# Attention scores: the correction product on 64 rows of the array, two heads on its two row halves

## The chip, the cores and the metric

The kernel runs on one core of a Trainium2 chip. Its time is the device time of one execution in microseconds (us); the median of three executions stands for the kernel. The profiled execution has a time of its own, which lies near that median.

The engines are named as in the profile: PE is TensorE's matmul and PEld its load of the stationary operand, DVE is VectorE, ACT is ScalarE, POOL is GpSimd, SP issues most DMAs.

## The reference, cut to what matters

The model has two layers over 256 latent and 256 context tokens of width 1024. Each layer has a mixer of three branches (attention, a state-space scan, retention) and an MLP. The change concerns the attention branch: 8 query heads of width 64, in two groups of four, and each group shares one key and one value head.

```python
q = rms_norm(aq.reshape(b, l, ATTN_HEADS, ATTN_HEAD_DIM), q_norm)      # then rotary, for latent tokens
s = jnp.einsum('bqkgd,bskd->bkgqs', qblk, k, preferred_element_type=jnp.float32) * scale
p = jax.nn.softmax(s, axis=-1).astype(v.dtype)
return jnp.einsum('bkgqs,bskd->bqkgd', p, v)
```

Context tokens attend to the 256 context tokens, latent tokens to all 512. Layer 0 computes all four blocks of 128 query tokens, layer 1 (the last) only the two latent blocks.

## The kernel before, in words

All matrix products take their operands as two parts, a high part rounded to fp32r and the low part that remains. A weight product is then three matmuls (high x high, low x high, high x low), at lines L256 to L258 and, for the projection of q, L268 to L270. These make up most of TensorE's work.

For the scores the two parts of a query head (64 + 64 values) are put on the 128 rows of the array together. `prep_q` (L540) rounds q (L555, ACT), subtracts (L556, DVE), and transposes the pair through the array (L559) to `qT_`: for each head 64 rows of high part and, below them, 64 rows of low part. `prep_k` lays the keys' high part twice over each other (`kT_[:, g, 0]`), and likewise their low part (`kT_[:, g, 1]`). So a head's scores for a block of 128 queries are two matmuls (L633) into one PSUM bank, both on all 128 rows: the first is (q high + q low) x k high, the second (q high + q low) x k low.

`att(g)` (L612) runs one group. A step is one PSUM bank of 512 score columns: one head with 512 keys, or two heads (`u` = 0, 1) with 256 keys. For each step `front` (L628) issues the matmuls, DVE takes the row maximum (L636), ACT the exponential (L640), DVE the division (L645). `back` transposes the probabilities through the array (L655) and ACT copies them to SBUF (L657, L659). `value` multiplies them with v (L670): two heads at a time on the two column halves of the array, 64 columns each (`tile_position=(0, 64 * j)`), in plain f32. The loop at L677 issues `front` of step n, `value` of step n - 4, `back` of step n - 3.

PSUM has eight banks: three rotate under the name `gps` for the weight products, four under `mps` for everything in attention, one is `xps`.

The order of the instructions on each engine is not that of the code. A scheduler places them when the program is built: by the order in which they were issued, by its own reckoning of when operands and buffers are ready, and so that TensorE always has something; between the steps of attention it puts weight products (z, the second q, x). At run time each engine goes through its list in that fixed order.

The places that the change touches: the split of q at L555 and L556, the list of steps at L624 and L625, and the matmuls of `front` at L630 to L634.

Of the kernel before, what the change touches and what calls it, by code (L numbers as in the profile page):

```python
# [10 lines left out]
F32R = mybir.dt.float32r  # L11
I32 = mybir.dt.int32
AF = mybir.ActivationFunctionType
ALU = mybir.AluOpType
# [78 lines left out]
def build(nc, tc, h0, cc, cr, wm, wg, wt, wk, ws, cols, rep, cst, cst2, out, taps=None):  # L93
    taps = taps or {}
    ctx = ExitStack()
    with ctx:
# [8 lines left out]
        V, A, PE = nc.vector, nc.scalar, nc.tensor  # L105
# [5 lines left out]
        def gps(shape):  # L111
            return gp.tile([P, 512], F32, tag="g", name="gps")
# [4 lines left out]
        def mps():  # L117
            return mp.tile([P, 512], F32, tag="m", name="mps")
# [25 lines left out]
        def rpv(l, nm):  # L144
            o, w = REPS[nm]
            return rp[:, l * NREP + o:l * NREP + o + w]
# [74 lines left out]
        def split(hi, lo, src):  # L221
            W["cp"] = A.copy(hi, src)  # L222
            return V.tensor_tensor(lo, src, hi.bitcast(F32), ALU.subtract)  # L223
# [131 lines left out]
        with tc.tile_pool(name="st", bufs=1, reuse_waits="tile") as stp:  # L355
# [33 lines left out]
            ps = mps()  # L389
# [55 lines left out]
        for l in range(DEPTH):  # L445
# [8 lines left out]
            with ExitStack() as lctx:  # L454
# [6 lines left out]
                def bt(shape, tag, bufs=1, dt=F32):  # L461
                    return bp.tile(shape, dt, tag=tag, name=tag, bufs=bufs)

                def mt(shape, name, dt=F32):
                    n = 4 * math.prod(shape[1:])
                    c = 4 if n > 2048 else 2 if n > 1024 else 1
                    return bp.tile(shape, dt, tag=f"m{c}", name=name, bufs=NB[c])

                def art(n, name, dt=F32):
                    return bp.tile([P, n], dt, tag="ar", name=name, bufs=2)  # L470
# [8 lines left out]
                kT_ = art(2048, "kT", F32R).rearrange("p (g x s) -> p g x s", g=2, x=2)  # L479
                qT_ = cp.tile([P, 8, T], F32R, tag="hm", name="qT")  # L480
# [59 lines left out]
                def prep_q(g, i, rsq):  # L540
                    ps = qps[g][i]
                    pv = ps.rearrange("p (a b c) -> p a b c", a=2, b=4)
                    sq = mt([P, 8, 64], "sqq")
                    A.activation(sq, ps.rearrange("p (a c) -> p a c", a=8), AF.Square)
                    V.reduce_sum(rsq[:, 8 * i:8 * i + 8], sq, AX.X)
                    qr = mt([P, 2, 4, 64], "qr")
                    if qt[2 * i] < 2:
                        V.tensor_tensor(qr.rearrange("p a b c -> p (a b) c"), pv.rearrange("p a b c -> p (a b) c"),
                                        rpv(l, "qn").unsqueeze(1).to_broadcast([P, 8, 64]), ALU.mult)
                    else:  # L550
                        t2 = mt([P, 2, 4, 64], "t2")
                        rope64(pv, cw[:, 0], 4, sq.rearrange("p (a b) c -> p a b c", a=2), t2, qr)
                    for a_ in range(2):
                        q2 = mt([P, 4, 2, 64], "q2")
                        A.copy(q2[:, :, 0, :].bitcast(F32R), qr[:, a_])  # L555
                        V.tensor_tensor(q2[:, :, 1, :].bitcast(F32R), qr[:, a_], q2[:, :, 0, :], ALU.subtract)  # L556
                        ps = mps()
                        for j in range(4):
                            PE.transpose(ps[:, j * 128:j * 128 + 128], q2[:, j].rearrange("p a b -> p (a b)"), ident)  # L559
                        o = (2 * i + a_) * 128  # L560
                        A.copy(qT_[:, 4 * g:4 * g + 4, o:o + 128], ps.rearrange("p (j s) -> p j s", j=4))
# [27 lines left out]
                ps = mps()  # L589
# [22 lines left out]
                def att(g):  # L612
                    rsq = bt([P, 16], "rsq")
                    for i in range(nt // 2):
                        prep_q(g, i, rsq)
                    sq_, rsq = rsq, bt([P, 16], "rsr", 2)
                    nsc = bt([P, 16], "nsc", 2)
                    rsqrt(rsq[:, 0:4 * nt], sq_[:, 0:4 * nt], nsc[:, 0:4 * nt], 1.0, 64 * EPS)
                    V.tensor_scalar(nsc[:, 0:4 * nt], rsq[:, 0:4 * nt], -1.0, None, ALU.mult)
                    steps = []  # L620
                    for i in range(nt):
                        nk = 256 if qt[i] < 2 else 512
                        nh = 512 // nk
                        for jp in range(2):  # L624
                            steps += [(i, jp, s_, nk, nh) for s_ in range(2 // nh)]  # L625
                    st = {}

                    def front(i, jp, s_, nk, nh):  # L628
                        j0 = 2 * jp + s_
                        ps = mps()  # L630
                        for u in range(nh):
                            for x in range(2):
                                PE.matmul(ps[:, u * nk:u * nk + nk], qT_[:, 4 * g + j0 + u, i * 128:i * 128 + 128],  # L633
                                          kT_[:, g, x, 0:nk], start=x == 0, stop=x == 1)  # L634
                        mx = bt([P, 8], "mx", 6)
                        V.reduce_max(mx[:, 0:nh], ps.rearrange("p (u k) -> p u k", u=nh), AX.X)  # L636
                        V.tensor_tensor(mx[:, 2:2 + nh], mx[:, 0:nh], nsc[:, 4 * i + j0:4 * i + j0 + nh], ALU.mult)
                        pr = mt([P, T], "pr")
                        for u in range(nh):
                            A.activation(pr[:, u * nk:u * nk + nk], ps[:, u * nk:u * nk + nk], AF.Exp,  # L640
                                         bias=mx[:, 2 + u:3 + u], scale=rsq[:, 4 * i + j0 + u:4 * i + j0 + u + 1],
                                         accum_out=mx[:, 4 + u:5 + u])
                        V.reciprocal(mx[:, 6:6 + nh], mx[:, 4:4 + nh])
                        for u in range(nh):
                            V.tensor_scalar(pr[:, u * nk:u * nk + nk], pr[:, u * nk:u * nk + nk],  # L645
                                            mx[:, 6 + u:7 + u], None, ALU.mult)
                        st[i, jp, s_] = pr

                    def back(i, jp, s_, nk, nh):
                        if s_ == 0:  # L650
                            st["pT", jp] = mt([P, 4, 2, 128], "pT")
                        pT, pr = st["pT", jp], st.pop((i, jp, s_))
                        pt = mps()
                        for c in range(4):
                            PE.transpose(pt[:, c * 128:c * 128 + 128], pr[:, c * 128:c * 128 + 128], ident)  # L655
                        if nh == 1:
                            A.copy(pT[:, :, s_], pt.rearrange("p (c s) -> p c s", s=128))  # L657
                        else:
                            A.copy(pT[:, 0:2].rearrange("p c u s -> p u c s"),  # L659
                                   pt.rearrange("p (u c s) -> p u c s", u=2, c=2))  # L660
                        return pT

                    def value(i, jp, s_, nk, nh):
                        ncn = nk // 128
                        if s_ < 2 // nh - 1 or jp == 0:
                            return
                        po = mps()[:, 0:256]
                        for c in range(ncn):
                            for j in range(2):
                                PE.matmul(po[64 * j:64 * j + 64], vt[:, c, 64 * g:64 * g + 64],  # L670
                                          st["pT", j][:, c].rearrange("p u s -> p (u s)"), start=c == 0, stop=c == ncn - 1,
                                          tile_position=(0, 64 * j))
                        split(brh[:, 2 * g:2 * g + 2, i * 128:i * 128 + 128],
                              brl[:, 2 * g:2 * g + 2, i * 128:i * 128 + 128],
                              po.rearrange("p (u s) -> p u s", u=2))

                    for n in range(len(steps) + ALAG + VLAG):  # L677
                        if n < len(steps):
                            front(*steps[n])
                        if n >= ALAG + VLAG:  # L680
                            value(*steps[n - ALAG - VLAG])
                        if ALAG <= n < len(steps) + ALAG:
                            back(*steps[n - ALAG])
# [398 lines left out]
            with ExitStack() as lctx:  # L1082
# [35 lines left out]
                for i in range(7):  # L1118
                    ps = gps(None)
# [39 lines left out]
                for half in range(2):  # L1159
# [11 lines left out]
                    for i in range(i0, 16):  # L1171
                        ps = gps(None)
# [3 lines left out]
                    for i in range(8):  # L1176
# [18 lines left out]
                        else:  # L1195
                            ps = gps(None)
                            for kk in range(2):
                                fm(l, ("w2", half, i, kk), hhf[kk][0], hhf[kk][1], 8, ps[:, 0:nq],
                                   start=kk == 0, stop=kk == 1)
# [138 lines left out]
```

## Time and profile before

| | before |
|---|---|
| median of 3 executions | 1448.71 us (1448.47 to 1449.59) |
| profiled execution, its own time | 1447.74 us |
| span of its trace | 1445.9 us |
| PE busy | 1430.7 us, 99% of the span |
| DVE busy | 1011.8 us, 70% |
| ACT busy | 664.4 us, 46% |
| chain that ended last, by engine | PE 94%, DVE 3%, DMA 1%, ACT 1% |

The span runs from the first to the last instruction; what lies around it is 1.8 us. A matmul's duration in the trace is longer than the time after which the next one starts, since matmuls are pipelined. What a matmul costs in a row of them is therefore read from the distance between two starts and not from its duration, and a PE that is called busy can still be waiting for some tenths of a microsecond.

### The profile page before, as it was taken

To read this page: it belongs to the slowest core of one execution; us is meant where nothing else is said; L and a number is where in the kernel's file an instruction comes from. 1 tells how busy PE (TensorE), PEld (TensorE's weight loads), DVE (VectorE), ACT (ScalarE), POOL (GpSimd) and SP (SyncE) were. 2 spreads that over 40 slices of the span, in tenths; PEclk is the share of its full clock that TensorE was granted. 3 is DMA by queue.
4 is the path that set the end of the run, shared out by engine and by line. 5 is a ranking of instruction groups with operands and counts; after the bars stand their busy time and mean duration, and the time that the engine had idled before them with its cause. 6 is when DMAs were issued, how large, how long until landed. Compare 5 with 4: busy or idle time off the path is not lost.

```text
span 1445.9 us, 22592 instructions
## 1 busy us (share of the span) xinstructions
PE 1430.7 (99%) x8790; PEld 1236.2 (85%) x8790; DVE 1011.8 (70%) x2003; ACT 664.4 (46%) x1170; POOL 61.9 (4%) x118
## 2 busy tenths in 40 slices
PE   8999999999999999999999999999999999999997
PEld 6877777888888889888888888987988999999997
DVE  5778589598866767895456644797985876765664
ACT  4577567242322335442224323576663444663563
POOL 0000010000000000000001100000000020000000
PEclk9999999999999999999999999999999999999999
DMA  9411344354025582564545634232443466655551
GB/s 355 184 45 44 102 121 107 125 180 161 30 95 167 165 315 75 174 214 136 161 156 192 195 115 139 88 123 73 140 132 102 132 228 222 207 189 181 186 188 60
DMA packets 66107, 217.07 MB, mean 150 GB/s; under 512 B 7600, under 2 KB 10032, under 8 KB 65872
## 3 DMA queue, kind: packets, MB, share of 16 engines
q1 hardware_dynamic: 53264, 170.99, 35.4%
q0 software_dynamic: 12736, 44.64, 9.8%
q8 instruction: 69, 1.13, 0.3%
q14 instruction: 38, 0.31, 0.1%
HBM read 213.44 MB, written 2.16 MB: 149 GB/s over the span
## 4 chain that ended last, share of the span: by engine, by line
PE 94%; DVE 3%; DMA 1%; ACT 1%; issue 0%; SPq 0%; DVEq 0%
PE gps L258 23%; PE gps L256 23%; PE gps L257 23%; PE mps L951 2%; PE mps L953 2%; PE mps L952 2%; PE mps L670 2%; PE mps L633 1%; PE mps L655 1%; DMA R<-drow 1%; PE mps L765 1%; PE gps L951 1%; PE gps L952 1%; PE gps L953 1%; PE mps L975 1%; DVE wl L223 1%
## 5 line engine op out<-in xcount | busy, mean ns | idle before, releaser
L222 ACT CAST wh<-raw 128x1024 fp32r<-128x1024 f32 (+1 forms) x284 | 297.3, 1049 | 554.2 <-PE gps L257 452.8
L223 DVE TENSOR_TENSOR wl<-raw,wh 128x1024 fp32r<-128x1024 f32 (+1 forms) x284 | 347.2, 1225 | 236.8 <-ACT wh L222 235.2
L256 PE MATMUL gps<-uh,wh 128*128 128x256 f32 (+1 forms) x1304 | 442.5, 340 | 0.6 <-DVE sz L691 0.3
L258 PE MATMUL gps<-uh,wl 128*128 128x256 f32 (+1 forms) x1304 | 442.6, 340 | 0.1
L257 PE MATMUL gps<-ul,wh 128*128 128x256 f32 (+1 forms) x1304 | 442.3, 339 | 0.0
L256 PEld LDWEIGHTS gps<-uh,wh 128*128 128x128 f32 x1304 | 246.4, 189 | 28.1 <-issue 1.5
L258 PEld LDWEIGHTS gps<-uh,wl 128*128 128x128 f32 x1304 | 246.7, 189 | 27.6 <-issue 2.1
L257 PEld LDWEIGHTS gps<-ul,wh 128*128 128x128 f32 x1304 | 246.6, 189 | 26.5 <-issue 0.7
L258 PE MATMUL gps<-hh__5331,wl 128*128 128x512 f32 (+1 forms) x272 | 102.6, 377 | 0.0
L256 PE MATMUL gps<-hh__5331,wh 128*128 128x512 f32 (+1 forms) x272 | 102.5, 377 | 0.0
L257 PE MATMUL gps<-hl__5332,wh 128*128 128x512 f32 (+1 forms) x272 | 102.4, 377 | 0.0
L216 DVE CUSTOM_DVE_ANT_0 mraw<-mraw,crow,cl 128x1024 f32<-128x1024 f32 x64 | 82.0, 1282 | 1.1
L1104 DVE SCALAR_TENSOR_TENSOR h<-gps,mod,h 128x256 f32<-128x256 f32 x48 | 21.9, 481 | 72.2 <-PE gps L258 72.2
L256 PE MATMUL gps<-hh__11889,wh 128*128 128x256 f32 x256 | 72.3, 282 | 0.0
L258 PE MATMUL gps<-hh__11889,wl 128*128 128x256 f32 x256 | 72.2, 282 | 0.0
L257 PE MATMUL gps<-hl__11890,wh 128*128 128x256 f32 x256 | 72.1, 282 | 0.0
L257 PE MATMUL gps<-brl,wh 128*128 128x512 f32 (+1 forms) x192 | 65.7, 342 | 0.0
L258 PE MATMUL gps<-brh,wl 128*128 128x512 f32 (+1 forms) x192 | 65.6, 341 | 0.0
L256 PE MATMUL gps<-brh,wh 128*128 128x512 f32 (+1 forms) x192 | 65.2, 340 | 0.0
L257 PEld LDWEIGHTS gps<-hl__5332,wh 128*128 128x128 f32 x272 | 51.2, 188 | 9.5
L256 PEld LDWEIGHTS gps<-hh__5331,wh 128*128 128x128 f32 x272 | 51.2, 188 | 9.5
L258 PEld LDWEIGHTS gps<-hh__5331,wl 128*128 128x128 f32 x272 | 51.2, 188 | 9.3
(326 smaller groups left out, 2319.8 us busy)
## 6 DMA issues: line engine op xcount, KB each, us to landing
raw<-in_ws_dram SPq DMA_DIRECT2D x280, 512.0 KB, 3.5
mraw<-in_wt_dram POOLq DMA_DIRECT2D x62, 512.0 KB, 3.6
mraw<-in_wm_dram SPq DMA_DIRECT2D x16, 512.0 KB, 10.1
R<-drow POOLq DMA_DIRECT2D x24, 256.0 KB, 4.7
h<-in_h_dram SPq DMA_DIRECT2D x16, 256.0 KB, 5.8
graw<-in_wg_dram SPq DMA_DIRECT2D x16, 256.0 KB, 5.6
graw<-in_wg_dram POOLq DMA_DIRECT2D x16, 256.0 KB, 9.7
raw<-in_wk_dram SPq DMA_DIRECT2D x4, 544.0 KB, 5.3
```

Source lines behind the costliest of these rows:

```text
L216: V.tensor_tensor_reduce(o, r, crow[:, v], 0.5, col(l, "bm")[:, cb:cb + 1], ALU.mult, ALU.add, mods[l][:, cb, v:v + 1])
L222: W["cp"] = A.copy(hi, src)
L223: return V.tensor_tensor(lo, src, hi.bitcast(F32), ALU.subtract)
L256: PE.matmul(ps, a, xh(k), start=start and k == 0, stop=False)
L257: PE.matmul(ps, a, xl(k), start=False, stop=False)
L258: W["mm"] = PE.matmul(ps, b, xh(k), start=False, stop=stop and k == K - 1)
L633: PE.matmul(ps[:, u * nk:u * nk + nk], qT_[:, 4 * g + j0 + u, i * 128:i * 128 + 128], kT_[:, g, x, 0:nk], start=x == 0, stop=x == 1)
L670: PE.matmul(po[64 * j:64 * j + 64], vt[:, c, 64 * g:64 * g + 64], st["pT", j][:, c].rearrange("p u s -> p (u s)"), start=c == 0, stop=c == ...
L951: PE.matmul(ps, a, wa, start=kc == 0, stop=False)
L952: PE.matmul(ps, b, wa, start=False, stop=False)
L953: PE.matmul(ps, a, wb, start=False, stop=kc == 7)
L1104: W["dv"] = V.scalar_tensor_tensor(h[:, i, a:b], ps[:, a - q0:b - q0], coef[:, i, v:v + 1], h[:, i, a:b], ALU.mult, ALU.add)
```

## The change

The high and low parts of q no longer lie in the same order for all heads. Of the four heads of a group, heads 0 and 1 keep the high part on rows 0 to 63; heads 2 and 3 have it on rows 64 to 127, below the low part. For that, each split of four heads on ACT and on DVE becomes two splits of two heads.

The second product (against k low) takes the high part of q alone: 64 rows, with `tile_position=(64 * p, 0)`, so on the upper half of the array for heads 0 and 1 (p = 0) and on the lower half for heads 2 and 3 (p = 1). The term q low x k low is left out of the scores. The steps are reordered so that a head of the first pair and one of the second alternate, and `front` of the first of them issues the products of both, into two PSUM banks: first product of p = 0, of p = 1, second product of p = 0, of p = 1.

```diff
--- before.py
+++ after.py
@@ -552,8 +552,11 @@
                         rope64(pv, cw[:, 0], 4, sq.rearrange("p (a b) c -> p a b c", a=2), t2, qr)
                     for a_ in range(2):
                         q2 = mt([P, 4, 2, 64], "q2")
-                        A.copy(q2[:, :, 0, :].bitcast(F32R), qr[:, a_])
-                        V.tensor_tensor(q2[:, :, 1, :].bitcast(F32R), qr[:, a_], q2[:, :, 0, :], ALU.subtract)
+                        for jp in range(2):
+                            js = slice(2 * jp, 2 * jp + 2)
+                            A.copy(q2[:, js, jp, :].bitcast(F32R), qr[:, a_, js])
+                            V.tensor_tensor(q2[:, js, 1 - jp, :].bitcast(F32R), qr[:, a_, js], q2[:, js, jp, :],
+                                            ALU.subtract)
                         ps = mps()
                         for j in range(4):
                             PE.transpose(ps[:, j * 128:j * 128 + 128], q2[:, j].rearrange("p a b -> p (a b)"), ident)
@@ -621,17 +624,25 @@
                     for i in range(nt):
                         nk = 256 if qt[i] < 2 else 512
                         nh = 512 // nk
-                        for jp in range(2):
-                            steps += [(i, jp, s_, nk, nh) for s_ in range(2 // nh)]
+                        for s_ in range(2 // nh):
+                            steps += [(i, jp, s_, nk, nh) for jp in range(2)]
                     st = {}
 
                     def front(i, jp, s_, nk, nh):
                         j0 = 2 * jp + s_
-                        ps = mps()
-                        for u in range(nh):
-                            for x in range(2):
-                                PE.matmul(ps[:, u * nk:u * nk + nk], qT_[:, 4 * g + j0 + u, i * 128:i * 128 + 128],
-                                          kT_[:, g, x, 0:nk], start=x == 0, stop=x == 1)
+                        if jp == 0:
+                            st["ps"] = [mps(), mps()]
+                            for u in range(nh):
+                                for p in range(2):
+                                    PE.matmul(st["ps"][p][:, u * nk:u * nk + nk],
+                                              qT_[:, 4 * g + 2 * p + s_ + u, i * 128:i * 128 + 128],
+                                              kT_[:, g, 0, 0:nk], start=True, stop=False)
+                                for p in range(2):
+                                    r = slice(64 * p, 64 * p + 64)
+                                    PE.matmul(st["ps"][p][:, u * nk:u * nk + nk],
+                                              qT_[r, 4 * g + 2 * p + s_ + u, i * 128:i * 128 + 128],
+                                              kT_[r, g, 1, 0:nk], start=False, stop=True, tile_position=(64 * p, 0))
+                        ps = st["ps"][jp]
                         mx = bt([P, 8], "mx", 6)
                         V.reduce_max(mx[:, 0:nh], ps.rearrange("p (u k) -> p u k", u=nh), AX.X)
                         V.tensor_tensor(mx[:, 2:2 + nh], mx[:, 0:nh], nsc[:, 4 * i + j0:4 * i + j0 + nh], ALU.mult)
```

In the changed program L637 is the first product, L642 the second, L562 the transpose of q, L666 that of the probabilities, L681 the value product; weight products keep their lines. The rows of order below are of PE and in the program's order; an `mps` number is one step's PSUM bank, and the two numbers of a pair are the two heads' banks.

The scores of the first two query blocks in layer 0, first group (256 keys, two heads per bank), before:

```order
L559 MATMUL mps_770<-cs_73,q2_767 128x128 x4
L633 MATMUL mps_790<-kT_601,qT_602 128x256 x4
L633 MATMUL mps_804<-kT_601,qT_602 128x256 x4
L633 MATMUL mps_818<-kT_601,qT_602 128x256 x4
L633 MATMUL mps_832<-kT_601,qT_602 128x256 x4
L257 MATMUL gps_1154<-ul_82,wh_1156 128x512
```

and of the change:

```order
L562 MATMUL mps_778<-cs_73,q2_773 128x128 x4
L637 MATMUL mps_798<-kT_601,qT_602 128x256
L637 MATMUL mps_799<-kT_601,qT_602 128x256
L642 MATMUL mps_798<-kT_601,qT_602 128x256
L642 MATMUL mps_799<-kT_601,qT_602 128x256
L637 MATMUL mps_798<-kT_601,qT_602 128x256
L637 MATMUL mps_799<-kT_601,qT_602 128x256
L642 MATMUL mps_798<-kT_601,qT_602 128x256
L642 MATMUL mps_799<-kT_601,qT_602 128x256
L637 MATMUL mps_826<-kT_601,qT_602 128x256
```

Here the two products on 64 rows of a pair follow each other, each time between products on 128 rows.

Layer 0, first group, a later query block with 512 keys; before, from one step's scores to the next one's:

```order
L633 MATMUL mps_853<-kT_601,qT_602 128x512 x2
L269 MATMUL gps_1204<-wh_1192,ul_82 128x256
L270 MATMUL gps_1204<-wl_1193,uh_81 128x256
L268 MATMUL gps_1204<-wh_1192,uh_81 128x256
L269 MATMUL gps_1204<-wh_1192,ul_82 128x256
L655 MATMUL mps_864<-cs_73,pr_812 128x128 x4
L270 MATMUL gps_1204<-wl_1193,uh_81 128x256
L268 MATMUL gps_1204<-wh_1192,uh_81 128x256
L269 MATMUL gps_1204<-wh_1192,ul_82 128x256
L270 MATMUL gps_1204<-wl_1193,uh_81 128x256
L268 MATMUL gps_1204<-wh_1192,uh_81 128x256
L633 MATMUL mps_870<-kT_601,qT_602 128x512 x2
```

and of the change, one pair:

```order
L666 MATMUL mps_896<-cs_73,pr_839 128x128 x4
L637 MATMUL mps_902<-kT_601,qT_602 128x512
L642 MATMUL mps_902<-kT_601,qT_602 128x512
L268 MATMUL gps_1212<-wh_1200,uh_81 128x256
L269 MATMUL gps_1212<-wh_1200,ul_82 128x256
L270 MATMUL gps_1212<-wl_1201,uh_81 128x256
L637 MATMUL mps_903<-kT_601,qT_602 128x512
L642 MATMUL mps_903<-kT_601,qT_602 128x512
L268 MATMUL gps_1212<-wh_1200,uh_81 128x256
L269 MATMUL gps_1212<-wh_1200,ul_82 128x256
```

Here the scheduler has put the second product of a head directly behind its first, and weight products between the two heads, so that each product on 64 rows stands alone between products on 128 rows.

Layer 1, first group, the first two pairs; before:

```order
L559 MATMUL mps_8177<-cs_73,q2_8174 128x128 x4
L633 MATMUL mps_8197<-kT_8031,qT_8032 128x512 x2
L633 MATMUL mps_8207<-kT_8031,qT_8032 128x512 x2
L633 MATMUL mps_8217<-kT_8031,qT_8032 128x512 x2
L633 MATMUL mps_8227<-kT_8031,qT_8032 128x512 x2
L258 MATMUL gps_8750<-uh_81,wl_8753 128x512
L256 MATMUL gps_8750<-uh_81,wh_8752 128x512
```

and of the change:

```order
L562 MATMUL mps_8197<-cs_73,q2_8192 128x128 x4
L637 MATMUL mps_8217<-kT_8047,qT_8048 128x512
L637 MATMUL mps_8218<-kT_8047,qT_8048 128x512
L642 MATMUL mps_8217<-kT_8047,qT_8048 128x512
L642 MATMUL mps_8218<-kT_8047,qT_8048 128x512
L637 MATMUL mps_8237<-kT_8047,qT_8048 128x512
L637 MATMUL mps_8238<-kT_8047,qT_8048 128x512
L642 MATMUL mps_8237<-kT_8047,qT_8048 128x512
L642 MATMUL mps_8238<-kT_8047,qT_8048 128x512
L256 MATMUL gps_8774<-uh_81,wh_8776 128x512
```

Here the products on 64 rows stand in twos again.

Over the whole program there are 24 pairs, 8 with 256 columns and 16 with 512. The two products on 64 rows are neighbours in 7 of the 8 and in 5 of the 16. That makes 12 neighbouring pairs and 24 single products, so 36 places where PE goes from products on 128 rows to products on 64 rows and back; none of them lies next to a column-tiled value product. The places where PE goes to products on 64 columns and back (the value product and two products of the scan) are 38 before and 39 in the change. The lists of SP and POOL are the same in both; those of ACT and DVE differ in and just behind the attention stages.

## Rows read from the trace of the kernel before

**Rows 1.** The page: busy time, share of the span and instructions of each engine.

```profile
PE 1430.7 (99%) x8790; PEld 1236.2 (85%) x8790; DVE 1011.8 (70%) x2003; ACT 664.4 (46%) x1170; POOL 61.9 (4%) x118
```

**Rows 2.** Busy time by stretch: the attention stages of layer 0 and layer 1.

```profile
core 0: us, PE busy (x) PEld busy (x) DVE busy (x) ACT busy (x) POOL busy (x), PEclk, DMA share, GB/s
70.00:150.00 80.00, 80.00 (x494) 62.26 (x493) 61.88 (x174) 55.43 (x129) 0.82 (x2) 1.00 0.14 46
940.00:1005.00 65.00, 64.98 (x405) 51.92 (x404) 54.59 (x150) 46.99 (x94) 1.21 (x3) 1.00 0.26 84
```

**Rows 3.** Waits of PEld, 70 to 150 us: total us, times, longest.

```profile
PEld mps L670 <- ACT pT L659: 1.1, 3, 0.4
...
PEld mps L633 <- ACT pr L640: 0.3, 1, 0.3
```

**Rows 4.** Timeline of PE, 978.3 to 981.6 us: start, duration, instruction.

```profile
978.33 0.39 PE L257 MATMUL gps<-ul,wh 128*128 128x512 f32 x1
978.55 0.40 PE L258 MATMUL gps<-uh,wl 128*128 128x512 f32 x1
978.88 1.94 PE L670 MATMUL mps<-pT,c 128*64 128x256 f32 x14
980.75 0.51 PE L256 MATMUL gps<-uh,wh 128*128 128x512 f32 x1
981.09 0.39 PE L257 MATMUL gps<-ul,wh 128*128 128x512 f32 x1
981.32 0.40 PE L258 MATMUL gps<-uh,wl 128*128 128x512 f32 x1
```

**Rows 5.** Timeline of PE from 105.0 us, in two windows.

```profile
105.05 0.43 PE L670 MATMUL mps<-pT,c 128*64 128x256 f32 x1
...
105.32 0.38 PE L670 MATMUL mps<-pT,c 128*64 128x256 f32 x1
105.63 0.39 PE L269 MATMUL gps<-wh,ul 128*128 128x256 f32 x1
105.85 0.28 PE L270 MATMUL gps<-wl,uh 128*128 128x256 f32 x1
105.97 0.28 PE L268 MATMUL gps<-wh,uh 128*128 128x256 f32 x1
```

**Rows 6.** Timeline of PEld in the stretch of rows 4.

```profile
978.33 0.19 PEld L258 LDWEIGHTS gps<-uh,wl 128*128 128x128 f32 x1
978.87 1.49 PEld L670 LDWEIGHTS mps<-pT,c 128*64 128x64 f32 x14 [0.36 <-issue]
980.75 0.19 PEld L256 LDWEIGHTS gps<-uh,wh 128*128 128x128 f32 x1 [0.39 <-issue]
```

**Rows 7.** Timeline of PE, a whole value product, 100.9 to 103.05 us.

```profile
101.13 1.95 PE L670 MATMUL mps<-pT,c 128*64 128x256 f32 x16
103.01 0.33 PE L655 MATMUL mps<-cs,pr 128*128 128x128 f32 x1
```

**Rows 8.** Timeline of PE, scores in a row: 256 columns, then 512.

```profile
120.64 1.23 PE L633 MATMUL mps<-kT,qT 128*128 128x256 f32 x8
121.71 0.39 PE L257 MATMUL gps<-ul,wh 128*128 128x512 f32 x1
...
956.58 2.08 PE L633 MATMUL mps<-kT,qT 128*128 128x512 f32 x8
958.50 0.39 PE L258 MATMUL gps<-uh,wl 128*128 128x512 f32 x1
```

**Rows 9.** Groups by line and shape, whole span: busy us, mean ns, idle before.

```profile
L633 PE MATMUL mps<-kT,qT 128*128 128x512 f32 x64 | 21.0, 425 | 0.0
L633 PE MATMUL mps<-kT,qT 128*128 128x256 f32 x32 | 4.6, 290 | 0.0
L640 ACT ACTIVATE pr<-mps,mx,rsr 128x512 f32<-128x512 f32 x32 | 24.8, 782 | 5.4 <-DVE mx L637 3.4 <-PE mps L633 1.8
L640 ACT ACTIVATION_READ_ACCUMULATOR pr<-mps,mx,rsr 128x1 f32 x48 | 9.9, 205 | 0.0
L555 ACT CAST q<-qr 128x256 fp32r<-128x256 f32 x12 | 4.4, 407 | 6.6 <-DVE rsr L295 3.0 <-DVE qr L548 2.6 <-DVE qr L513 1.1
L556 DVE TENSOR_TENSOR q<-qr,q 128x256 fp32r<-128x256 f32 x12 | 4.6, 420 | 0.5 <-ACT q L555 0.5
```

## The prediction

> **What bounds the kernel now.** I read the page first: PE is busy 99% of the span, DVE 70%, ACT 46% [rows 1]. Then the attention stages by themselves, since only they change: in both, PE is busy from end to end at the full clock, while DVE is busy 61.88 of 80 us and 54.59 of 65, ACT 55.43 of 80 and 46.99 of 65 [rows 2]. In the waits of that stretch PE's loads wait for ACT by some tenths of a microsecond: 1.1 us in three waits for copied probabilities, 0.3 us once before a score [rows 3]. So the weight products put between the steps cover the latency of the softmax, and each stage lasts as long as PE needs for its list. What the change costs or gives is the difference of PE's own list. Neither ACT nor DVE sets the end there.
>
> "Busy" hides what I need next, so I read distances between starts in the timeline. A 512-column weight product is followed by the next one after 0.22 to 0.23 us (978.33 to 978.55, 981.09 to 981.32) [rows 4], a 256-column one after 0.12 us (105.85 to 105.97) [rows 5]. Scores in a row go at the same pace: 8 with 512 columns in 1.92 us, 8 with 256 columns in 1.07 us, the first of each with its load in front [rows 8].
>
> **The price of leaving and re-entering the full array.** The value product is the place to read it: it runs on two column halves of 64.
> - Entry: the 512-column product ahead of it is followed after 0.33 us, not 0.23 (978.55 to 978.88) [rows 4]: 0.10 us.
> - Return: one half's two records start at 105.05 and 105.32, and the next full product at 105.63 [rows 5]. A whole value product, 16 records on two halves, takes 1.88 us [rows 7], so 14 more records cost 1.88 - 0.58 = 1.30 us. If the halves run side by side these are 6 more steps of 0.217 us; one after the other the 16 would need 3.5 us. So the halves do run side by side. The last record took 0.31 us instead of 0.22: 0.09 us for the return.
> - Loads: normally a load begins one matmul early. At a switch it begins with its own matmul: at 980.75 both start together, after 0.39 us in which no load ran [rows 4, 6]. The first full product afterwards takes 0.34 us (980.75 to 981.09) instead of 0.23 [rows 4], so 0.11 us for a stationary operand of 128 columns. For one of 64 columns it is 0.05 us (0.27 instead of 0.22) [rows 5].
>
> **The change part by part.**
> - Single products on 64 rows. The trace has no product on 64 rows. The low end for one is nothing: it streams the same columns as before, so there is no gain either. The high end, the nearest rows, is the price of the column halves with a stationary operand of 128 columns: 0.10 entry + 0.11 load + 0.09 return + 0.11 load of the next = 0.41 us. I take the high end, because the array is cut into tiles there as here, and every switch in these rows shows it.
> - The order pieces of the change show 36 places where PE goes to 64 rows and back: 24 single products, 12 neighbouring pairs. 36 x 0.41 = 14.8 us.
> - Neighbouring pairs. There the second product runs beside the first, as the column halves do [rows 7], and its time goes: 5 pairs of 512 columns by 0.23 us and 7 of 256 columns by 0.12 us, together 2.0 us. The bounds are 2.0 us and nothing. I take 2.0 us. Should the pair's two loads come one after the other, 12 x 0.11 = 1.3 us come back.
> - The reordered steps make one more visit to the column halves (39 for 38): 0.10 + 0.05 + 0.09 + 0.11 = 0.35 us.
> - The split of q: 12 more instructions each on ACT and DVE. The whole ones take 407 and 420 ns [rows 9]; a half costs between half and all of that, so the extra is 0 to 4.9 us on ACT and 0 to 5.0 us on DVE. I price it at nothing, as the weight products that PE runs meanwhile hide it; both engines have some 10 us or more to spare in each stage [rows 2]. Without that cover it would be up to 0.4 us for each of the 12 places, since the transpose waits for it: 4.9 us.
> - Two banks at once. A pair takes two of the four banks of attention, so its second head's first product can wait for the exponential that frees the bank. The order piece with 512 columns shows weight products ahead of it, which cover such a wait; I price it at nothing and keep it as a rival.
> - SP's and POOL's lists are the same. Everything behind the stages is only later, by what PE is later.
>
> Sum: 14.8 - 2.0 + 0.35 = 13.1 us. On the profiled execution's 1447.74 us that gives 1460.9 us. The median of the runs is 0.97 us above the profiled execution, so I predict 1461.8 us.
>
> The Trainium skill bears on the one thing that no row shows. Its page "TensorEngine Tiling (Array Packing)", section Tiling Modes, Key Properties, says that changing the mode, not just the tile, drains TensorE, and names 64 x 128 among the modes; rows 4 and 5 agree for columns, no run here shows it for rows. By that rule the switch has its price; without it the sum would be the first rival's. The same page's table of theoretical speedup gives up to 2x for a contraction of at most 64, which speaks for the change; by it all 24 pairs together would save 4.6 us, but the order parts 12 of them.
>
> **The rivals.**
> 1. The switch to row halves costs nothing: the load of a product on 64 rows goes ahead as any other does, and nothing has to leave the array first. For it: the columns keep their places, only the rows are halved, and the switches in the rows are all between column widths. Against it: every change of the tiles that the rows show is paid, at entry and at return [rows 4, 5]. The 24 single products then cost nothing, the 12 pairs save 2.0 us, the extra visit costs 0.35 us: -1.65 us, 1447.1 us. This is the side that is not slower. It decides where a place costs less than 0.13 us: 36 of them then stay under 4.6 us, and the time under 1451.6 us, 0.2% above before.
> 2. Only the emptying of the array is paid, and the loads go ahead: 36 x (0.10 + 0.09) = 6.8 us, so 6.8 - 2.0 + 0.35 = 5.2 us, 1453.9 us. For it: a load of 64 rows touches half of the array. Against it: at every switch in the rows the loads come late [rows 5, 6].
> 3. The banks: at the 16 pairs with 512 columns PE stands before the second head's first product until an exponential frees its bank. That instruction takes 782 ns and its accumulator 205 ns [rows 9]; with half of that at each pair, 16 x 0.5 = 8 us are added to the sum: 1469.8 us. For it: such a wait is there before already, 0.3 us once [rows 3]. Against it: the scheduler parted 11 of the 16 pairs, which keeps PE at work.
>
> **How the numbers follow.** My forecast has a chance of 0.62, with its own range of 1459 to 1465 us (pairs that do not run side by side and loads one after the other above it, the smallest steps of the rows below it). Rival 1 has 0.14, rival 2 has 0.12, rival 3 has 0.12. The range of 1452 to 1467 us holds the forecast, rival 2 and about half of rival 3; left out are rival 1 and the other half, 0.20. What a measurement of this kernel can tell from no change is about 0.2%, 2.9 us. Faster than 1445.8 us would need rival 1 with a gain in the order of the waits besides: 0.02. Within 0.2% is the rest of rival 1: 0.12. Slower is all else: 0.86.
>
> **What would show it.** In the profile of the changed kernel: the distance from a 512-column product to a following product on 64 rows (0.33 us if right, 0.23 if rival 1 holds); from a single product on 64 rows to the next full one (0.23 + 0.11 + 0.09, about 0.43 us); from that one on (0.34 us). The two starts of a neighbouring pair lie within some hundredths of a microsecond of each other if they run side by side, 0.2 us apart if not. PE's distances should account for about 13 us in the two attention stages and nothing elsewhere, with ACT and DVE still less than fully busy there. Waits of PEld for the exponential, at L637, of several microseconds in all would mean rival 3. A time under 1452 us would make the price of the switch wrong, one above 1467 us the priced-at-nothing terms.

## The result, and the profile after

| | before | changed |
|---|---|---|
| median | 1449.0 us (1448.47 to 1449.59, 4 runs) | 1461.99 us (1461.16 to 1462.42, 4 runs) |
| profiled execution / span of its trace | 1447.74 / 1445.9 us | 1462.42 / 1460.6 us |

The ratio is 1.0094, 95% interval [1.0083, 1.0106]: slower, by 13.0 us in the medians. The forecast was 1461.8 us.

The page of the changed kernel, busy time by engine, answers to [rows 1].

```profile
PE 1444.2 (99%) x8790; PEld 1235.5 (85%) x8790; DVE 1011.9 (69%) x2015; ACT 666.6 (46%) x1182; POOL 61.9 (4%) x118
```

The reader is to see that the number of matmuls is the same, and PE's busy time is 13.5 us more, while its loads, DVE and ACT have hardly moved (two of them with 12 more instructions). So the time is PE's own. A busy PE can hide short waits, so these are read by themselves at the end of this section.

Where the stages lie shows it too. Four weight products, one each from ahead of the attention of layer 0, from 340 us, from 940 us and from the end, in PE's timeline of the kernel before and then of the changed kernel:

```profile
68.34 0.40 PE L256 MATMUL gps<-uh,wh 128*128 128x512 f32 x1
340.50 0.39 PE L256 MATMUL gps<-uh,wh 128*128 128x512 f32 x1
938.96 0.28 PE L256 MATMUL gps<-uh,wh 128*128 128x256 f32 x1
1435.52 0.28 PE L256 MATMUL gps<-hh__11889,wh 128*128 128x256 f32 x1
```

```profile
69.09 0.40 PE L256 MATMUL gps<-uh,wh 128*128 128x512 f32 x1
350.61 0.39 PE L256 MATMUL gps<-uh,wh 128*128 128x512 f32 x1
949.09 0.28 PE L256 MATMUL gps<-uh,wh 128*128 128x256 f32 x1
1450.18 0.28 PE L256 MATMUL gps<-hh__11913,wh 128*128 128x256 f32 x1
```

The same product starts 0.8 us later than before just ahead of the attention of layer 0 (the start of the program, whose loads scatter by about that much), 10.1 us later at 340 us, still 10.1 us later at 940 us, and 14.7 us later at the end. All of the rest of the loss is in and just behind the two attention stages: 9.4 us in layer 0 and 4.5 us in layer 1, 13.9 us together.

The timeline of PE in the changed kernel, around one single product on 64 rows (L642; start, duration, instruction), answers to [rows 4]:

```profile
94.97 0.39 PE L637 MATMUL mps<-kT,qT 128*128 128x512 f32 x1
95.29 0.49 PE L642 MATMUL mps<-kT,qT 64*128 64x512 f32 x1
95.71 0.39 PE L268 MATMUL gps<-wh,uh 128*128 128x256 f32 x1
95.94 0.28 PE L269 MATMUL gps<-wh,ul 128*128 128x256 f32 x1
```

From the product on 128 rows to that on 64 it is 0.32 us instead of 0.23, from there to the next full product 0.42 instead of 0.23, and that one with 256 columns takes 0.23 instead of 0.12 us. The price of this place is 0.09 + 0.19 + 0.11 = 0.39 us, for the 0.41 us of the sum. What makes it up is seen in the loads. The timeline of PEld at another single product, answering to [rows 6]:

```profile
972.91 0.19 PEld L637 LDWEIGHTS mps<-kT,qT 128*128 128x128 f32 x1
973.34 0.18 PEld L642 LDWEIGHTS mps<-kT,qT 64*128 64x128 f32 x1 [0.24 <-issue]
973.77 0.19 PEld L257 LDWEIGHTS gps<-ul,wh 128*128 128x128 f32 x1 [0.25 <-issue]
973.88 0.19 PEld L258 LDWEIGHTS gps<-uh,wl 128*128 128x128 f32 x1
```

and the matmuls that belong to them:

```profile
972.93 0.48 PE L637 MATMUL mps<-kT,qT 128*128 128x512 f32 x1
973.34 0.50 PE L642 MATMUL mps<-kT,qT 64*128 64x512 f32 x1
973.77 0.50 PE L257 MATMUL gps<-ul,wh 128*128 128x512 f32 x1
974.11 0.40 PE L258 MATMUL gps<-uh,wl 128*128 128x512 f32 x1
```

At both changes the load begins together with its own matmul (973.34, 973.77), after 0.24 and 0.25 us in which no load ran. Only the next load (973.88) is ahead of its matmul again (974.11). The first step is 0.41 us here and not 0.32, because the product on 128 rows stands behind transposes and its own load is late too (972.91 for 972.93); a first score behind transposes takes 0.31 to 0.34 us in the kernel before, so that part is not new. A neighbouring pair, in PE's timeline:

```profile
968.41 0.73 PE L637 MATMUL mps<-kT,qT 128*128 128x512 f32 x2
969.07 0.49 PE L642 MATMUL mps<-kT,qT 64*128 64x512 f32 x2
969.50 0.50 PE L256 MATMUL gps<-uh,wh 128*128 128x512 f32 x1
969.83 0.40 PE L257 MATMUL gps<-ul,wh 128*128 128x512 f32 x1
```

Both products on 64 rows are done in 0.43 us (969.07 to 969.50), the same as one by itself: the second starts 3 to 4 ns after the first in every neighbouring pair. The return and the next load are paid as for a single one.

The split of q and the banks, in the groups and the waits (70 to 155 us) of the changed kernel:

```profile
L557 ACT CAST q<-qr 128x128 fp32r<-128x128 f32 x24 | 5.6, 295 | 7.9 <-DVE rsr L295 4.3 <-DVE qr L513 2.4 <-DVE qr L548 1.2
L558 DVE TENSOR_TENSOR q<-qr,q 128x128 fp32r<-128x128 f32 x24 | 5.6, 281 | 0.0
...
PEld mps L642 <- issue: 4.1, 15, 0.4
PEld mps L637 <- ACT pT L668: 0.7, 2, 0.4
```

The halves take 295 and 281 ns, so the split costs 1.2 us more of ACT's busy time (5.6 us for 4.4) and 1.0 us more of DVE's (5.6 for 4.6) [rows 9]. The idle time of the loads ahead of L642 is put down to issue: nobody is waited for, the load just does not go ahead. The waits for ACT at L637 are 0.7 us in layer 0, for a copy of probabilities. In layer 1 (940 to 1020 us) they are 0.6 us for the copy of q and, for the exponential that frees a bank:

```profile
PEld mps L637 <- ACT pr L651: 0.2, 1, 0.2
```

That is 1.5 us in all, 0.2 us of it for the exponential, against the 8 us that the rival of the banks needed.

### The profile page after: what moved, and what is told of

Same layout as the page of the kernel before. It is cut to its first block, busy times and chain, and to the rows that moved or that the text cites. A ratio compares the mean times of both kernels' runs of the same rounds, so it can differ in the third digit from the quotient of the medians.

```text
span 1460.6 us, 22611 instructions
## 1 busy us (share of the span) xinstructions
PE 1444.2 (99%) x8790; PEld 1235.5 (85%) x8790; DVE 1011.9 (69%) x2015; ACT 666.6 (46%) x1182; POOL 61.9 (4%) x118
## 4 chain that ended last, share of the span: by engine, by line
PE 92%; DVE 4%; DMA 2%; ACT 1%; issue 1%; SPq 0%; POOL 0%; DVEq 0%; ACTq 0%
PE gps L258 23%; PE gps L257 23%; PE gps L256 23%; PE mps L681 2%; PE mps L964 1%; PE mps L962 1%; PE mps L963 1%; DMA raw<-in_wk_dram 1%; PE mps L666 1%; PE mps L642 1%; DVE wl L223 1%; PE mps L637 1%; PE mps L776 1%; PE gps L962 1%; PE gps L964 1%; PE gps L963 1%
## 6 DMA issues: line engine op xcount, KB each, us to landing
mraw<-in_wm_dram SPq DMA_DIRECT2D x16, 512.0 KB, 10.1
```

## The experiments

Each was timed against runs of the kernel before on the same chip; ratios are to these. Where a time "from the attention on" is given, it is read as above, from the profiled executions: how much later the same weight product starts at the end than just ahead of the attention, in comparison with the kernel before.

**The second product on all 128 rows again.** The rest of the change stays.

```diff
-                                    r = slice(64 * p, 64 * p + 64)
-                                              qT_[r, ...], kT_[r, g, 1, 0:nk], ..., tile_position=(64 * p, 0))
+                                              qT_[:, ...], kT_[:, g, 1, 0:nk], ...)
```

> The changed kernel with its second product on all 128 rows again (q low x k low is back in the scores); the split of q, the alternating steps and the two banks taken at once stay. 36 places with 64 rows become none. Theory (each place where TensorE goes to 64 rows and back costs 0.41 us, the rest of the change next to nothing): before plus one more visit to the column halves, 0.35 us, so about 1449.4 us against 1449.0. Rival (the reordered steps, the pair of banks and the two-part split of q take the time): about 1460 us.

Measured 1450.38 us, ratio 1.0015 [1.0006, 1.0023]. Most of the loss goes with the products on 64 rows: the reordered steps, the two banks and the split of q together cost 1 to 3 us (1.6 us from the attention on) and not 11. They cost somewhat more than the 0.35 us expected; the fifth experiment shows a part of why.

**All pairs neighbours.**

```diff
+                                with tc.issue_after(f_.ins):    # f_: the last first product
                                     for p in range(2):
                                         r = slice(64 * p, 64 * p + 64)
                                         PE.matmul(...)
```

> The changed kernel with the second products queued behind the first product of both heads, so that the two products on 64 rows are neighbours in all 24 pairs: 24 places for 36, and 38 visits to the column halves as before. Theory: 24 x 0.41 = 9.8 us, less 16 x 0.23 + 8 x 0.12 = 4.6 us for products that run beside their partner, so +5.2 us over before, 1454.2 us. Rival (the price goes with the 48 products on 64 rows or with the rearrangement, and not with the places): about 1462 us as in the changed kernel. In the trace the two starts of a pair lie 3 to 4 ns apart in all 24 pairs.

Measured 1453.44 us, ratio 1.0044 [1.0030, 1.0058]. With the same 48 products on 64 rows, half of the loss is gone: 6.4 us by the ratio, for 13.6 us in the changed kernel. By the sum, 12 places fewer are 4.9 us of that, and 12 more second products beside their partner are 2.6 us (11 of 512 columns, one of 256). So the price does not go with the number of products; this run alone does not part the places from the sharing, and the run with neighbours on the same half prices the sharing. From the attention on it is 5.2 us above before, the sum to a tenth. All 24 pairs start 3 to 4 ns apart.

**One visit a query block.**

```diff
-                        if jp == 0:
-                            st["ps"] = [mps(), mps()]
...
+                        ns = 2 // nh
+                        if jp == 0 and s_ == 0:
+                            st["ps"] = [[mps(), mps()] for _ in range(ns)]
+                            hs_ = [(s2, u, p) for s2 in range(ns) for u in range(nh) for p in range(2)]
+                            for s2, u, p in hs_:
+                                f_ = PE.matmul(st["ps"][s2][p][:, u * nk:u * nk + nk],
...
+                            with tc.issue_after(f_.ins):
+                                for s2, u, p in hs_:
...
```

The first loop issues all first products of the block, the second all its products on 64 rows.

> All first products of a query block, then all its second products on 64 rows, two pairs in one visit: 12 places for 36, 36 visits to the column halves for 38. With 512 keys a block takes all four banks of attention at once. Theory: 12 x 0.41 = 4.9 us, less 4.6 us, less 2 x 0.35 = 0.7 us: -0.4 us against before, 1448.6 us. Rival (banks): with all four banks taken PE waits at each of the 8 blocks with 512 keys for one or two exponentials of 0.99 us, 8 to 16 us more, 1457 to 1465 us, with waits of PEld for ACT at the first product that sum to as much.

Measured 1449.74 us, ratio 1.0009 [1.0000, 1.0017]. The timeline of PE shows one visit: four products on 64 rows, two pairs, in 0.67 us.

```profile
90.99 0.39 PE L638 MATMUL mps<-kT,qT 128*128 128x512 f32 x1
91.31 0.73 PE L644 MATMUL mps<-kT,qT 64*128 64x512 f32 x4
91.98 0.38 PE L269 MATMUL gps<-wh,ul 128*128 128x256 f32 x1
```

The loss is gone to within 0.2%, but there is no gain: 12 visits cost about as much as all pairs give back. The rival of the banks fell as to its size, though something of it is there. The waits of PEld for the exponential, at the transpose of the probabilities, in this kernel and then in the kernel before (both 70 to 160 us), are:

```profile
PEld mps L668 <- ACT pr L653: 2.5, 7, 0.6
```

```profile
PEld mps L655 <- ACT pr L640: 0.6, 2, 0.4
```

They are 1.9 us more. Whether they are why the ratio's 1.3 us lies 1.7 us above the -0.4 us expected is not shown, for the profiled execution was late for another reason. From 21 to 25 us, long before the attention and with PE's list still the same as before, the granted clock fell for a part of the time to the lower of its two levels, 1.2 GHz. In the kernel before, and then in this one:

```profile
21.00:25.00 4.00, 4.00 (x41) 3.28 (x40) 2.33 (x7) 1.28 (x3) 0.00 (x0) 1.00 1.05 402
21.00:25.00 4.00, 3.95 (x19) 3.95 (x20) 2.75 (x8) 1.04 (x3) 0.00 (x0) 0.57 1.05 399
```

The mean granted clock is 0.57 for 1.00, and PE ran 19 matmuls for 41. Not long before, PE had stood for 1.01 us for a DMA, but in the kernel before for 1.14 us, so why the clock fell in one and not in the other is open. The first and the last of the four weight products above, in this kernel:

```profile
70.71 0.40 PE L256 MATMUL gps<-uh,wh 128*128 128x512 f32 x1
1437.88 0.28 PE L256 MATMUL gps<-hh__11913,wh 128*128 128x256 f32 x1
```

They are 2.4 us later than before ahead of the attention and 2.4 us at the end, so from the attention on this kernel takes as long as the kernel before. With the 0.78 us that the fifth experiment gives for each of the two visits to the column halves that are gone, the sum is -1.3 us, so about 1.3 us are left that these waits can explain; that they do was not tried. How much of the 1.3 us by the ratio comes from such starts, the record does not show.

**Neighbours on the same half.**

```diff
-                                        r = slice(64 * p, 64 * p + 64)
-                                        PE.matmul(..., tile_position=(64 * p, 0))
+                                        r = slice(0, 64)
+                                        PE.matmul(..., tile_position=(0, 0))
```

In this kernel q also lies high part first for all heads (those lines are left out here).

> As e2_neighbours (24 places, all pairs neighbours), but both products of a pair on the upper 64 rows, and q laid high part first for all heads. Theory (a pair's second product is free because it runs on the other half of the array): the 4.6 us come back, 1454.2 + 4.6 = 1458.8 us, and the starts of a pair are 0.22 us apart with 512 columns. Rival (neighbours are cheap because they share one visit, whichever rows they use): as e2_neighbours, about 1454.2 us.

Measured 1457.67 us, ratio 1.0073 [1.0060, 1.0086], 4.2 us above the kernel with neighbours on both halves (5.7 us from the attention on), for the 4.6 us expected. The timeline of PE shows a pair on one half:

```profile
977.55 0.73 PE L643 MATMUL mps<-kT,qT 64*128 64x512 f32 x2
978.21 0.55 PE L667 MATMUL mps<-cs,pr 128*128 128x128 f32 x3
```

It takes 0.66 us where the pair on two halves took 0.43. So the 2.0 us of the sum were for products that truly run beside each other, and not for sharing a visit. The starts were 0.33 to 0.34 us apart with 512 columns, where 0.22 was expected: the first one's load is not hidden, which adds 0.11 us.

**The value product begins with the last copy, in the kernel before.**

```diff
-                            for j in range(2):
+                            for j in (1, 0):
                                 PE.matmul(po[64 * j:64 * j + 64], ...
```

> The kernel before with one edit: the value product begins with the head pair whose probabilities are copied last, so that nothing later parts its matmuls. The places where TensorE goes to the column halves and back become 30 for 38; the scores are as before. Theory (each such place costs 0.35 us whatever is computed there): 8 x 0.35 = 2.8 us less than the 1449.0 us of before, 1446.2 us. Rival (the parted value products filled time in which PE would have waited for the copy): no change, 1449 us, with longer waits of PEld for ACT at the value product.

Measured 1441.90 us, ratio 0.9964 [0.9952, 0.9977]: faster than both kernels, and about twice the gain expected (5.2 us, with an interval of 3.3 to 7.0 us). The rival fell: the waits for ACT's copies at the value product from 70 to 150 us did not grow (1.4 us for 2.0). Why the gain is larger: before, a parted value product is one matmul of one half (two records) by itself and the rest later. In the kernel before, the rest of the product that begins in [rows 5], PE's timeline:

```profile
106.30 1.94 PE L670 MATMUL mps<-pT,c 128*64 128x256 f32 x14
108.17 0.39 PE L270 MATMUL gps<-wl,uh 128*128 128x256 f32 x1
```

and a whole one in the kernel of this experiment:

```profile
100.56 1.95 PE L670 MATMUL mps<-pT,c 128*64 128x256 f32 x16
102.44 1.82 PE L655 MATMUL mps<-cs,pr 128*128 128x128 f32 x14
```

The parted product takes 0.58 us for its first two records and 1.87 us for the other 14; the whole one takes 1.88 us for 16. A half that runs without its partner saves nothing for the other, so parting costs 0.57 us inside the visits, and 0.10 + 0.11 us for one more entry and load: 0.78 us. Eight of them are 6.2 us. Besides, two of the whole value products before contained a wait. The longer, in the kernel before:

```profile
141.73 2.29 PE L670 MATMUL mps<-pT,c 128*64 128x256 f32 x16
143.95 0.33 PE L655 MATMUL mps<-cs,pr 128*128 128x128 f32 x1
```

It takes 2.22 us; the other takes 1.94 us, and all eight with 512 keys take 1.88 us in this kernel: 0.4 us more. Together that is 6.6 us, which is what the profiled execution gains from the attention on, for the 5.2 us of the ratio.

**Both together.** The kernel with one visit a block, with that edit of the value product.

> e3_one_visit_a_block with the same edit of the value product: 12 places with 64 rows, 27 with column halves for the 38 of before. Theory: 12 x 0.41 - 4.6 = +0.3 us for the scores and 11 x 0.35 = 3.9 us less for the column halves: 1445.4 us. Rival (the banks: as the order parts less, PE has less to do while it waits for ACT): 1447 us or more.

Measured 1443.52 us, ratio 0.9973 [0.9963, 0.9983], so 3.9 us faster than before by the ratio, near the 3.6 us expected. The rival, 1447 us or more, fell. That the number fits is in part luck: it was priced at 0.35 us a visit, and with the 0.78 us that the experiment before gives for each of eight parted value products, and 0.35 us for three visits of the scan that are gone as well, the sum is a gain of 7.0 us. In the profiled execution the same two weight products are:

```profile
70.80 0.40 PE L256 MATMUL gps<-uh,wh 128*128 128x512 f32 x1
1432.87 0.28 PE L256 MATMUL gps<-hh__11913,wh 128*128 128x256 f32 x1
```

They are 2.5 us later than before and then 2.7 us earlier, so it gains 5.1 us from the attention on. What takes up the rest was not taken apart. The kernel does not beat the edit of the value product alone: the row halves give nothing on top of it.

## Why the prediction was right

- *PE's list sets the stages.* Right: DVE and ACT had room for the 12 instructions more, and the waits for them stayed within a few tenths of a microsecond each.
- *36 places at 0.41 us.* Right. The price was carried over from column halves to row halves, which no row of before showed; the rows after give the same steps (0.32 in, 0.42 out, 0.11 for the next load, at a 512-column product). The kernels with 36, 24 and no places lie 13.6, 6.4 and 2.2 us above before by their ratios; the step from 36 to 24 holds 2.6 us of sharing as well. The Trainium skill's page "TensorEngine Tiling (Array Packing)", Tiling Modes, Key Properties, says that changing the mode drains TensorE; the 0.09 to 0.10 us at each change agree with it for rows as for columns, though the emptying itself is not seen in a trace. The other half of the price is the 0.11 us of each of the two late loads.
- *12 pairs save 2.0 us.* Right, shown by the 3 to 4 ns between the starts, and by the 4.2 us that all 24 pairs are worth, for 4.6 by the same prices.
- *One more visit to the column halves, 0.35 us.* Mis-sized. The visit that was added is one more parted value product (nine for eight), which the fifth experiment puts at 0.78 us. With that the sum is 14.8 - 2.0 + 0.8 = 13.6 us, for 13.0 us measured in the medians, 13.6 by the ratio and 13.9 from the attention on. That the median came within 0.2 us of the forecast is luck, as the interval alone goes from 12.0 to 15.4 us; that it fell near 13 is not. The term was priced by the place alone; what the half without its partner loses was overlooked, although rows 5 and 7 held it.
- *The split of q and the banks at nothing.* Within what was measured: the kernel with full rows, which has them all, is 0.9 to 3.3 us slower than before, 0.8 us of it the parted product. Another 0.3 us are waits inside whole value products: of the three with 512 keys, in the kernel with full rows and in the changed one alike, the time above 1.88 us each is 0.75 us in all, before 0.42. How the rest falls to the split, the banks and the order was not taken apart.
- *The rivals.* A free switch and emptying alone both fell by the starts in the trace (0.32 and 0.42 us) and by the time. The banks fell for the change as it stands, and appeared as 1.9 us more of PEld's waits in layer 0 where four were taken at once; that these cost PE as much is not shown.

## What to carry to other kernels

Tiling the array pays only if what one visit saves is more than what the visit costs: here 0.41 us, against 0.23 us for a pair with 512 columns. Two pairs in one visit give back 0.46 us, and the kernel that has them so came out about even. So count the visits in the order that the scheduler has made, not in the code, and look whether partners are still neighbours there. Where a tiled product is already in use, begin it with the operand that is ready last, so that nothing parts it: one line, 0.36% here.

## What the runs showed of the hardware that was not expected

A product on one column half that has lost its partner costs twice: its visit, and the 0.43 us of its two steps, which the partner can no longer share; 0.78 us in all for one parted value product. On row halves the partners start 3 to 4 ns apart in the changed kernel, on column halves 6 to 7 ns. Neighbours on the same 64 rows take turns (0.66 us for a pair instead of 0.43). And the profiled executions of two kernels (one visit a block, and both together) lost 2.4 us at the start of the program, where PE's list is the same as before, in part to a granted clock of 0.57 for 1.00 over 4 us: a difference of that size in the time need not come from the edit.
